# Attention scores with keys on partitions, 256 queries at a time, and the maximum taken elementwise

## The chip, the cores and the metric

The program runs on one core of one Trainium2 chip. The metric is the device time of one execution in microseconds (us). The kernel before was timed three times: median 3153.96 us, from 3151.37 to 3155.75.

The engines are named as in the profile: PE is TensorE (matmul and transpose), PEld its weight load, DVE is VectorE, ACT is ScalarE, POOL is GpSimd, SP is the queue that issues the DMAs. SBUF is the core's working memory, PSUM the memory that PE writes to; POOL's operands all lie in SBUF here.

## The reference

Two layers work on 1024 latent tokens and 256 context tokens of width 1024: a bidirectional gated recurrence and a multi-head attention whose keys and values come from a common 128-wide latent. The change lies in the attention, 16 heads, 1024 queries against 1280 keys:

```python
s = einsum('bqhd,bkhd->bhqk', q_nope, k_nope) + einsum('bqhr,bkr->bhqk', q_pe, k_pe)
p = softmax(s * MLA_SCALE, axis=-1)
o = einsum('bhqk,bkhd->bqhd', p, v)
y = (o * silu(z)) @ w_out
```

All of it is in float32.

## The kernel before

A float32 value is kept as two numbers of a shorter format (fp32r), a high and a low part, made by `split` (L209): ACT casts the high part, DVE subtracts it to give the low part. A product of two such numbers is three matmuls (`mm3`, L262). The projections of keys and queries are folded together, so that scores are taken straight against the key latent: `kh` and `kl` are its two parts, `kr` the rotary part, and a head's folded queries are `qah`, `qal` with the rotary parts `rh`, `rl`.

The first layer takes the first 1.7 ms. Then come its output projection and the input projections of the attention (`mla_in`, L669, `mla_rope`, `mla_z`), and from about 2142 us to 2960 us the attention itself (`attend`, L929), followed by the output projection.

`attn_scores` (L838) works on one tile of 128 queries of one head, queries on partitions and the 1280 keys along the free axis in blocks of 512, 512 and 256. Each block is five matmuls into one PSUM buffer `s` (L854 to L858). DVE reduces each block to a maximum (L860, as a minimum, since the scale carries a minus) and the three to one (L866). ACT takes the exponential with that number as its bias and sums the row as it goes (L870), and DVE forms the reciprocal and scales the whole row of 1280 (L876 to L881).

`attn_values` (L884) takes two tiles of one head, which I call a unit: 16 heads times 4 make 64 units. The scaled probabilities have queries on partitions, but the product with the values needs keys there. So PE transposes them, four 128x128 pieces at a time, into a PSUM buffer `pt` (L901), ACT and DVE split each group out of PSUM into `ph` and `pl` (L906, recorded at L215 and L216), and `mm3` adds ten key tiles into `pv` (L914). The result is copied and split again (L919 to L921, the last step `ol` on POOL), multiplied with the head's value weights (L924), by the gate `z` on DVE (L926), and stored (L927).

`attn_prep` (L782) makes the folded queries of the next head meanwhile: small weight products (L799), every second head the transposes of the rotary parts (L817), two groups of six 512-wide matmuls (L833) with their splits. `tail` stands for the first half of the output projection's work on the first two tiles, used to fill the end.

What sets the order: `attend` sorts all these steps by due times, and PE is held to exactly that order (`AT_ORDER`, L1283). The other engines' instructions are ordered by a scheduler. Every engine executes its own list in order and waits at an instruction whose inputs or buffers aren't ready.

Of the kernel before, what the change touches and what calls it, by code (L numbers as in the profile page):

```python
# [18 lines left out]
P = 128  # L19
# [18 lines left out]
class Net:  # L38
# [630 lines left out]
    def mla_in(self, pool, pp, kp, a, hh, hl, st):  # L669
# [6 lines left out]
        for c in range(NT):  # L676
# [39 lines left out]
            )  # L716
            if lat:
# [64 lines left out]
    def attn_prep(self, pool, pp, a, st, qrD, zT, h, box):  # L782
# [23 lines left out]
        if h % 2 == 0:  # L806
# [6 lines left out]
            for b, n in self.qgs:  # L813
                sl = slice(b * P, (b + n) * P)
                ps = t(pp, [P, 512], F32, G_TAG)
                for j in range(n):
                    nc.tensor.transpose(ps[:, j * P : (j + 1) * P], qr[:, b + j], self.ident)  # L817
                for i, (rh, rl) in enumerate(box["pair"]):
                    own, twin = (slice(0, 64), slice(64, P))[:: 1 - 2 * i]
                    src = ps[own, : n * P]  # L820
                    nc.scalar.activation(rh[own, sl], src, AF.Copy, scale=SCALE)
# [16 lines left out]
    def attn_scores(self, pool, pp, st, box, i, prs):  # L838
        nc, t, NT = self.nc, self.t, self.NT
        mm = nc.tensor.matmul  # L840
        LK = NT * P
        blocks = [(o, min(512, LK - o)) for o in range(0, LK, 512)]
        nb = len(blocks)
        h, j = divmod(i, self.NL)
        qah, qal, rh, rl = box[h][:4]
        js = slice(j * P, (j + 1) * P)
        mx = t(pool, [P, 4], F32, "mx")
        sm = t(pool, [P, 4], F32, "sm")
        pr = t(pool, [P, LK], F32, "pr")
        sc = []  # L850
        for b, (o, w) in enumerate(blocks):
            s = t(pp, [P, 512], F32, "s")
            ks = slice(o, o + w)
            mm(s[:, :w], qah[:, js], st["kh"][:, ks], start=True, stop=False)  # L854
            mm(s[:, :w], qah[:, js], st["kl"][:, ks], start=False, stop=False)  # L855
            mm(s[:, :w], qal[:, js], st["kh"][:, ks], start=False, stop=False)  # L856
            mm(s[:, :w], rh[:, js], st["kr"][:, ks], start=False, stop=False)  # L857
            mm(s[:, :w], rl[:, js], st["kr"][:, ks], start=False, stop=True)  # L858
            with self.tc.high_priority(offset=AT_PRIO):
                nc.vector.tensor_reduce(mx[:, b : b + 1], s[:, :w], AX.X, ALU.min)  # L860
            sc.append(s)
            if b < nb - 1:
                yield
        nm = t(pool, [P, 1], F32, "nm")
        with self.tc.high_priority(offset=AT_PRIO):
            nc.vector.tensor_reduce(nm, mx[:, :nb], AX.X, ALU.min)  # L866
        for b, (o, w) in enumerate(blocks):
            yield
            with self.tc.high_priority(offset=EXP_PRIO):
                nc.scalar.activation(  # L870
                    pr[:, o : o + w], sc[b][:, :w], AF.Exp, bias=nm, scale=-1.0,
                    accum_out=sm[:, b : b + 1],
                )
        yield
        rs = t(pool, [P, 1], F32, "rs")
        nc.vector.tensor_reduce(rs, sm[:, :nb], AX.X, ALU.add)  # L876
        nc.vector.reciprocal(rs, rs)
        if i % NORM_ACT[1] < NORM_ACT[0]:
            nc.scalar.activation(pr, pr, AF.Copy, scale=rs)
        else:  # L880
            nc.vector.tensor_scalar(pr, pr, rs, None, ALU.mult)  # L881
        prs[i] = pr

    def attn_values(self, pool, pp, st, box, u, prs, yT):  # L884
        nc, t, NT = self.nc, self.t, self.NT
        tiles = [i for i in (2 * u, 2 * u + 1) if i < self.NH * self.NL]
        h, b = divmod(tiles[0], self.NL)
        n = len(tiles)
        N = n * P
        wvh, wvl, z = box[h][4:]  # L890
        np_ = -(-NT // 2)
        parts = {}
        acc = None
        for e in range(np_ + PV_LAG):
            if e < np_:
                m = min(2, NT - 2 * e)
                tp = t(pp, [P, 2, 2 * P], F32, "pt")
                for c in range(m):
                    for j, i in enumerate(tiles):
                        k = 2 * e + c  # L900
                        nc.tensor.transpose(  # L901
                            tp[:, c, j * P : (j + 1) * P], prs[i][:, k * P : (k + 1) * P], self.ident
                        )
                ph = t(pool, [P, 2, 2 * P], F32R, "ph")
                pl = t(pool, [P, 2, 2 * P], F32R, "pl")
                self.split(ph[:, :m, :N], pl[:, :m, :N], tp[:, :m, :N])  # L906
                parts[e] = (m, ph, pl)
            if e >= PV_LAG:
                if acc is None:
                    acc = self.pv[:, u % 2]  # L910
                m, ph, pl = parts.pop(e - PV_LAG)
                for c in range(m):
                    k = 2 * (e - PV_LAG) + c
                    self.mm3(acc[:, :N], st["vh"][:, k], st["vl"][:, k], ph[:, c, :N], pl[:, c, :N], k == 0, k == NT - 1)  # L914
            yield
        oh = t(pool, [P, 2 * P], F32R, "oh")
        ol = t(pool, [P, 2 * P], F32R, "ol")
        o32 = t(pool, [P, 2 * P], F32, "o32")
        nc.scalar.copy(o32[:, :N], acc[:, :N])  # L919
        nc.scalar.copy(oh[:, :N], o32[:, :N])  # L920
# [469 lines left out]
```

## Time and profile before

| | |
|---|---|
| median of three runs | 3153.96 us (3151.37 to 3155.75) |
| the profiled execution, time | 3156.2 us |
| the profiled execution, span | 3154.4 us |
| TensorE clock granted, mean | 0.994 |
| busy: PE, PEld, DVE, ACT, POOL | 3115.5, 2783.9, 2150.9, 1727.9, 255.8 us |
| instructions | 51488 |
| 2142 to 2960 us: PE, DVE, ACT, POOL busy | 813.5, 638.2, 507.7, 65.4 of 818 us |

The span runs from the first to the last instruction; the execution's own time is 1.8 us longer. A busy PE is not a PE at its peak: matmuls overlap, so the recorded length of one (0.28 us) is longer than the distance to the next (0.12 us), and a sum must be made with the distances.

### The profile page before, as it was taken

What the parts mean: (1) busy time and instruction counts of PE and PEld (TensorE: products, weight loads), DVE (VectorE), ACT (ScalarE), POOL (GpSimd) and SP (SyncE); (2) the same over time, 40 slices, a digit from 0 to 9 for tenths busy, and PEclk for the clock granted to TensorE, in tenths of its full rate; (3) what the DMA queues carried; (4) which work ended last, traced back from release to release, by engine and by line L of the source; (5) the groups of instructions that cost most, each with busy time, mean ns of one, the idle gap of its engine ahead of it and who ended that gap; (6) DMA issues with size and microseconds to landing.
All of it is one profiled execution on the core that took longest, in us unless ns stands there. A gap on an engine that the chain in (4) does not pass through costs nothing.

```text
span 3154.4 us, 51488 instructions
## 1 busy us (share of the span) xinstructions
PE 3115.5 (99%) x19412; PEld 2783.9 (88%) x19412; DVE 2150.9 (68%) x4853; ACT 1727.9 (55%) x4263; POOL 255.8 (8%) x350
## 2 busy tenths in 40 slices
PE   8899999999999999999999999999999999999999
PEld 7889989889898998988988788788999999999887
DVE  7777688776886758767585463536777777777642
ACT  5556465564655646555475563324666666666532
POOL 2000000000000000000001122210000000000000
PEclk8999999999999999999999999999999999999999
DMA  5110212102121021110127561430111011101261
GB/s 212 42 56 24 73 36 63 56 23 74 36 62 56 25 65 36 37 35 23 41 68 242 193 205 59 140 119 29 41 30 38 21 38 31 35 29 38 69 219 57
DMA packets 100010, 218.88 MB, mean 69 GB/s; under 512 B 10289, under 2 KB 47409, under 8 KB 99761
## 3 DMA queue, kind: packets, MB, share of 16 engines
q1 hardware_dynamic: 99760, 215.59, 21.0%
q8 instruction: 153, 2.51, 0.3%
q14 instruction: 97, 0.79, 0.1%
HBM read 175.70 MB, written 39.85 MB: 68 GB/s over the span
## 4 chain that ended last, share of the span: by engine, by line
PE 88%; DVE 4%; DMA 2%; issue 2%; ACT 2%; POOL 1%; SPq 0%; DVEq 0%; POOLq 0%; ACTq 0%
PE g L265 11%; PE g L264 11%; PE g L266 11%; PE lv L336 6%; PE pt L901 4%; PE o L487 3%; PE pv L264 2%; PE s L854 2%; PE pv L265 2%; PE pv L266 2%; PE s L855 2%; PE s L857 2%; PE s L858 2%; PE s L856 2%; PE lv L264 2%
## 5 line engine op out<-in xcount | busy, mean ns | idle before, releaser
L264 PE MATMUL g<-hh,wh 128*128 128x512 f32 (+1 forms) x1512 | 548.7, 363 | 0.8 <-DVE hh L254 0.6
L266 PE MATMUL g<-hl,wh 128*128 128x512 f32 (+1 forms) x1512 | 542.0, 360 | 2.7 <-DVE hl L255 2.6
L265 PE MATMUL g<-hh,wl 128*128 128x512 f32 (+1 forms) x1512 | 543.3, 359 | 0.0
L216 DVE TENSOR_TENSOR wl<-raw,wh 128x1024 fp32r<-128x1024 f32 (+1 forms) x170 | 209.7, 1236 | 174.0 <-ACT wh L215 163.7
L266 PEld LDWEIGHTS g<-hl,wh 128*128 128x128 f32 x1512 | 286.0, 189 | 39.3 <-DVE hl L255 3.6
L264 PEld LDWEIGHTS g<-hh,wh 128*128 128x128 f32 x1512 | 286.7, 190 | 37.6 <-DVE hh L254 0.9
L265 PEld LDWEIGHTS g<-hh,wl 128*128 128x128 f32 x1512 | 286.6, 190 | 35.7
L860 DVE TENSOR_REDUCE mx<-s 128x1 f32<-128x512 f32 (+1 forms) x384 | 229.3, 598 | 93.7 <-PE s L858 92.6
L870 ACT ACTIVATE pr<-s,nm 128x512 f32<-128x512 f32 (+1 forms) x384 | 232.3, 613 | 99.3 <-DVE nm L866 93.1
L336 PE MATMUL lv<-QX,KX 128*128 128x128 f32 x1920 | 264.4, 276 | 6.0 <-ACT QX L408 3.5
L336 PEld LDWEIGHTS lv<-QX,KX 128*128 128x128 f32 x1920 | 247.8, 193 | 15.2 <-ACT QX L408 4.4
L215 ACT CAST wh<-raw 128x1024 fp32r<-128x1024 f32 (+1 forms) x170 | 177.7, 1049 | 120.2 <-PE lv L265 42.1
L215 ACT CAST ph<-pt 128x512 fp32r<-128x512 f32 x320 | 187.6, 586 | 95.2 <-PE pt L901 85.2
L216 DVE TENSOR_TENSOR pl<-pt,ph 128x512 fp32r<-128x512 f32 x320 | 219.1, 685 | 12.5 <-ACT ph L215 12.4
L264 PE MATMUL g<-wh,hh 128*128 128x256 f32 (+2 forms) x676 | 197.7, 293 | 0.0
L264 PE MATMUL pv<-ph,vh 128*128 128x256 f32 x640 | 196.6, 307 | 0.0
L266 PE MATMUL g<-wl,hh 128*128 128x256 f32 (+2 forms) x676 | 196.4, 291 | 0.0
L901 PE MATMUL pt<-ident,pr 128*128 128x128 f32 x1280 | 191.8, 272 | 0.1
L265 PE MATMUL g<-wh,hl 128*128 128x256 f32 (+1 forms) x654 | 187.8, 287 | 0.0
L408 ACT COPY KX<-K 128x256 f32<-128x256 f32 (+1 forms) x288 | 109.6, 381 | 133.1 <-PE lv L336 75.9
L266 PE MATMUL pv<-pl,vh 128*128 128x256 f32 x640 | 180.0, 281 | 0.0
L265 PE MATMUL pv<-ph,vl 128*128 128x256 f32 x640 | 179.8, 281 | 0.0
(557 smaller groups left out, 7956.6 us busy)
## 6 DMA issues: line engine op xcount, KB each, us to landing
raw<-in_w_o SPq DMA_DIRECT2D x64, 512.0 KB, 4.2
raw<-in_w_qfbz SPq DMA_DIRECT2D x61, 512.0 KB, 3.8
raw<-in_ada_wT SPq DMA_DIRECT2D x32, 512.0 KB, 3.6
raw<-in_w_mo SPq DMA_DIRECT2D x24, 512.0 KB, 4.0
raw<-in_w_v SPq DMA_DIRECT2D x16, 512.0 KB, 3.6
yT<-Z SPq DMA_DIRECT2D x32, 256.0 KB, 2.0
raw<-in_w_z SPq DMA_DIRECT2D x16, 512.0 KB, 3.9
pyr<-yT SPq DMA_DIRECT2D x64, 128.0 KB, 3.9
```

Source lines behind the costliest of these rows:

```text
L215: nc.scalar.copy(hi, src)
L216: (eng or nc.vector).tensor_tensor(lo, src, v32(hi), ALU.subtract)
L264: mm(ps, lh, rh, start=first, stop=False)
L265: mm(ps, ll, rh, start=False, stop=False)
L266: mm(ps, lh, rl, start=False, stop=last)
L336: nc.tensor.matmul(ps[:, sl], lhs[:, sl], rhs[:, sl], start=True, stop=True)
L408: cp(m12(N[:]), m12(Y))
L487: nc.tensor.matmul(o[:, sl], l, r, start=i == 0, stop=i == len(ops) - 1)
L854: mm(s[:, :w], qah[:, js], st["kh"][:, ks], start=True, stop=False)
L860: nc.vector.tensor_reduce(mx[:, b : b + 1], s[:, :w], AX.X, ALU.min)
L870: nc.scalar.activation(pr[:, o : o + w], sc[b][:, :w], AF.Exp, bias=nm, scale=-1.0, accum_out=sm[:, b : b + 1],)
L901: nc.tensor.transpose(tp[:, c, j * P : (j + 1) * P], prs[i][:, k * P : (k + 1) * P], self.ident)
```

## The change

Scores are now computed with keys on partitions, for a whole unit of 256 queries at a time, so that the probabilities come out as the product with the values wants them. No transposes of probabilities are left.

- **Scores.** Ten key tiles in five PSUM buffers of 512 columns (two tiles of 256 queries each; four called `s`, one `s5`, each there once). Four passes are made first: `kh` with `qah`, `kl` with `qah`, `kh` with `qal`, `kr` with `rh`.
- **Maximum.** DVE takes the elementwise maximum over the five buffers (`m2`: one copy, four maxima of 128x512), then of its halves (`mf`, 128x256). PE transposes `mf` (two 128x128 pieces into `mt`), DVE reduces to one number for each query (`mr`), two matmuls with the identity spread it over a row, and ACT writes the negative into row 64 of the low rotary part `rl`.
- **Fifth pass.** A new operand `k5` holds the rotary keys in rows 0 to 63 and ones in row 64. The fifth pass, `k5` with `rl`, thus adds the low part and subtracts the maximum. It comes after the maximum is known.
- **Exponential and sums.** ACT takes the exponential of five buffers of 512 with no bias and no row sums. POOL adds the five up (four adds of 128x512, one of 128x256) to `l`; two float32 matmuls with a column of ones sum `l` over keys. Probabilities are no longer scaled; DVE takes the reciprocal `rc` of 128x2, SP writes it to DRAM (`lD`) and reads it back spread over all partitions (`rb`), and POOL multiplies the gated output `ya` by it.
- **Split.** `attn_split` makes `ph` and `pl` straight from the exponentials in SBUF.
- **Order.** `attend` is written out as a loop over units: scores of unit u, with splits of unit u-1 and the values of unit u-2 between them. DVE and ACT are now held to the written order too (`AT_HAND`).
- In `mla_in` ACT makes one more copy of 64x128 for each of ten key tiles.

The diff, cut to its core:

```diff
+            nc.scalar.copy(st["k5"][:64, sl], tp[:64, P : 2 * P])
...
+        for e in range(nb):
+            s = t(pp, [P, 512], F32, "s" if e < 4 else "s5")[:, : 2 * N].rearrange("p (a q) -> p a q", a=2)
+            for c in range(m):
+                for i, (l, r) in enumerate(((kh, qah), (kl, qah), (kh, qal), (kr, rh))):
+                    mm(o, l[:, ks], r[:, js], start=c + i == 0, stop=c == m - 1 and i == 3)
-                nc.vector.tensor_reduce(mx[:, b : b + 1], s[:, :w], AX.X, ALU.min)
+                    nc.vector.tensor_tensor(m2[:, :m], m2[:, :m], s[:, :m], ALU.max)
...
+                nc.vector.tensor_tensor(mf, m2[:, 0], m2[:, 1], ALU.max)
+            nc.tensor.transpose(mt[:, 0, j * P : (j + 1) * P], mf[:, j * P : (j + 1) * P], self.ident)
+            nc.vector.tensor_reduce(mr, mt[:, 0, :N].rearrange("p (j k) -> p j k", k=P), AX.X, ALU.max)
+            mm(mt[:, 1, j * P : (j + 1) * P], mr[:, j : j + 1].broadcast_to([P, P]), self.identr, ...)
+            nc.scalar.activation(rl[64:65, js], mt[64:65, 1, :N], AF.Copy, scale=-1.0)
+                mm(s[:, c], st["k5"][:, ks], rl[:, js], start=False, stop=c == m - 1, skip_group_check=True)
-                    pr[:, o : o + w], sc[b][:, :w], AF.Exp, bias=nm, scale=-1.0,
-                    accum_out=sm[:, b : b + 1],
+                nc.scalar.activation(p[:, :m], s[:, :m], AF.Exp)
+            add(l2, whole[0], whole[1], ALU.add)
+                add(l2, l2, p, ALU.add)
+            add(l, l2[:, 0], l2[:, 1], ALU.add)
...
-                        nc.tensor.transpose(
-                            tp[:, c, j * P : (j + 1) * P], prs[i][:, k * P : (k + 1) * P], self.ident
-                        )
-                self.split(ph[:, :m, :N], pl[:, :m, :N], tp[:, :m, :N])
+        self.split(ph[:, :m], pl[:, :m], p[:, :m])
...
+        nc.vector.reciprocal(rc, ps[:, 2 * P : 2 * P + n])
+        nc.sync.dma_start(row.rearrange("o (j p) -> p (o j)", p=P), rc)
+        nc.sync.dma_start(rb, row.broadcast_to([P, N]))
+        nc.gpsimd.tensor_tensor(y, y, rb, ALU.mult)
```

**DVE's list, before.** These are the rows of DVE over one tile of 128 queries, half a unit, in the middle of a head: block maxima `mx`, their minimum `nm`, sum and reciprocal `rs`, the scaling of the row `pr`, low parts `pl` taken from `pt` (PSUM) and `ph`.

```order
L860 TENSOR_REDUCE mx_27045<-s_27048 128x1
L926 TENSOR_TENSOR ya_27063<-pt_27059,za_5047_26022 128x256
L876 TENSOR_REDUCE rs_27055<-sm_26962 128x1
L877 RECIPROCAL rs_27055<-rs_27055 128x1
L881 TENSOR_SCALAR pr_26963<-pr_26963,rs_27055 128x1280
L216 TENSOR_TENSOR pl_27072<-pt_27066,ph_27071 128x512
L860 TENSOR_REDUCE mx_27045<-s_27081 128x1
L216 TENSOR_TENSOR pl_27094<-pt_27088,ph_27093 128x512
L860 TENSOR_REDUCE mx_27045<-s_27103 128x1
L866 TENSOR_REDUCE nm_27110<-mx_27045 128x1
```

**DVE's list, after.** These are the rows of DVE over one unit with no preparation of a next head in it: the running maximum `m` (the tile `m2`), its halves `mf`, the number for each query `mr`, and `pl`, now from `p` and `ph`, which both lie in SBUF.

```order
L864 COPY m_5172_27081<-s_27082 128x512
L862 TENSOR_TENSOR m_5172_27081<-m_5172_27081,s_27092 128x512
L862 TENSOR_TENSOR m_5172_27081<-m_5172_27081,s_27102 128x512
L216 TENSOR_TENSOR pl_27113<-p_27050,ph_27112 128x512
L862 TENSOR_TENSOR m_5172_27081<-m_5172_27081,s_27116 128x512
L216 TENSOR_TENSOR pl_27127<-p_27054,ph_27126 128x512
L862 TENSOR_TENSOR m_5172_27081<-m_5172_27081,s_5181_27130 128x512
L872 TENSOR_TENSOR mf_27141<-m_5172_27081 128x256
L216 TENSOR_TENSOR pl_27144<-p_27058,ph_27143 128x512
L878 TENSOR_REDUCE mr_27167<-mt_27140 128x2
L216 TENSOR_TENSOR pl_27170<-p_27062,ph_27169 128x512
L216 TENSOR_TENSOR pl_27174<-p_27066,ph_27173 128x512
```

Two low parts now stand between the block maxima, ahead of `mf`, and a third between `mf` and `mr`; the scaling of the rows is gone.

**POOL's list, before.** Over five units POOL has one `ol` for each and, every second head, the copies of the rotary part.

```order
L921 TENSOR_TENSOR ol_25320<-o_4881_25321,oh_25319 128x256
L825 COPY qrh_4905_25404<-qrh_4905_25404 64x512
L825 COPY qrh_4906_25405<-qrh_4906_25405 64x512
L921 TENSOR_TENSOR ol_25517<-o_4930_25518,oh_25516 128x256
L921 TENSOR_TENSOR ol_25691<-o_4970_25692,oh_25690 128x256
```

**POOL's list, after.** One unit: the sums `l` over the exponentials `p`, the product `ya` by the reciprocal `rb`, and `ol`.

```order
L903 TENSOR_TENSOR l_4986_26211<-p_26192,p_26196 128x512
L959 TENSOR_TENSOR ya_26177<-ya_26177,rb_26175 128x256
L905 TENSOR_TENSOR l_4986_26211<-l_4986_26211,p_26200 128x512
L943 TENSOR_TENSOR ol_26218<-o_4989_26219,oh_26217 128x256
L905 TENSOR_TENSOR l_4986_26211<-l_4986_26211,p_26204 128x512
L905 TENSOR_TENSOR l_4986_26211<-l_4986_26211,p_26208 128x512
L909 TENSOR_TENSOR l_26210<-l_4986_26211 128x256
```

The step that PE waits for at the head's value weights, `ol`, was alone on its engine. Now it stands behind two sums and behind `ya`, which waits for the DMA that brings `rb`.

More of the change, by code (lines that the diff above doesn't have):

```diff
@@ L916, in attn_values @@
[L916 to L920, printed above, removed]
[L921 removed]
+        acc = self.pv[:, u % 2]
+        k = 0
+        for m, ph, pl in cell["parts"]:
+            for c in range(m):
+                self.mm3(acc[:, :N], st["vh"][:, k], st["vl"][:, k], ph[:, c], pl[:, c], k == 0, k == NT - 1)
+                k += 1
+            yield
@@ L934, in attend @@
-        steps = []
+        units = [(h, b, min(2, NL - b)) for h in range(NH) for b in range(0, NL, 2)]
+        nb = -(-self.NT // 2)
+        per = -(-NL // 2)
+        prep = {}
         for h in range(1, NH):
-            t0 = NL * (h - 1) + 3 + AT_LAG
-            g = self.attn_prep(pool, pp, a, st, qrD, zT, h, box)
-            gap = min(0.9, (NL - 4 - AT_LAG) / 5)
-            steps += [(t0 + (e + (PREP_LATE if e > 1 and h % 2 == 0 else 0)) * gap, g) for e in range(6)]
-        nb = -(-self.NT * P // 512)
@@ L956 @@
+        for x in vals.values():
+            for _ in x:
+                pass
+        for _ in tail:
+            pass
 VEC = {}
```

237 lines of the change are left out of this document (144 added, 93 removed).

## Prediction

> **What bounds the kernel now.** I read the stages first (busy time in stretches), then the chain of waits inside a stretch of the attention, then the groups by line, then POOL and DVE in order of time, and last the DMA issues. In the stages, the columns are length, then busy time of PE, PEld, DVE, ACT and POOL, then granted clock and DMA:
>
> ```profile
> 2142.00:2960.00 818.00, 813.47 (x5524) 742.30 (x5523) 638.18 (x1361) 507.72 (x1306) 65.38 (x90) 1.00 0.10 31
> ```
>
> PE has no idle time to speak of in the attention, and POOL has little else. The chain of waits of 2446 to 2460 us, with its shares by line and some of its pieces (start, length, what), is PE alone:
>
> ```profile
> by line: PE pt L901 18.7%; PE s L856 10.8%; PE pv L266 10.3%; PE pv L264 10.2%; PE pv L265 10.2%; PE s L855 10.1%; PE s L854 9.9%; PE s L858 9.2%; PE s L857 9.2%; PE pt L266 0.9%; PE pt L264 0.8%; PE pt L265 0.8%
> ...
> 2446.18 0.12 PE s L858
> 2446.30 0.44 PE pt L901 x4
> 2446.74 0.12 PE pv L264
> ...
> 2447.46 0.23 PE s L854
> ```
>
> So a matmul of 256 columns holds PE for 0.12 us, one of 512 for 0.23, and a group of four transposes of probabilities for 0.44. POOL's `ol` comes once a unit and so gives the period (start, length, engine, line):
>
> ```profile
> 2343.16 0.73 POOL L921 TENSOR_TENSOR ol<-o,oh 128x256 fp32r<-128x256 f32 x1 [11.84 <-PE s L858]
> ...
> 2446.31 0.73 POOL L921 TENSOR_TENSOR ol<-o,oh 128x256 fp32r<-128x256 f32 x1 [11.82 <-PE s L858]
> 2458.22 0.74 POOL L921 TENSOR_TENSOR ol<-o,oh 128x256 fp32r<-128x256 f32 x1 [11.18 <-ACT oh L920]
> ```
>
> Two heads, eight units, take 2446.31 - 2343.16 = 103.15 us, 12.9 a unit; a unit without preparation of a head takes 11.9.
>
> **The change: PE.** All counts are per unit. The score passes are 30 matmuls before (2 tiles x 5 x (0.235 + 0.235 + 0.12) = 5.9 us, with 0.235 for the 512 columns) and 50 of 256 columns after (50 x 0.12 = 6.0): the columns are the same, and narrower passes cost 0.1 more. The other matmuls that stay are 30 for the values (3.6) and three for the head's value weights (0.36). Five groups of transposes go: 5 x 0.44 = 2.2. Together that makes 12.06 where the rows show 11.9, so the distances account for the unit. New are two transposes of `mf` (half a group, 0.22, up to 0.3 with the change of format), two matmuls of 128 columns that spread the maximum (bounded by two of 256 columns, 0.24), and the two sums by a column of ones. A float32 matmul counts as two instructions here. The nearest row is the two-column matmul of the start, 15 in 1.81 us:
>
> ```profile
> 39.85 1.81 PE L163 MATMUL lv<-csil,adap 128*128 128x2 f32 x15
> ```
>
> That is 0.12 each, four are 0.48. Net: -2.2 + 0.1 + 0.3 + 0.24 + 0.48 = -1.08 us a unit; a head's preparation is unchanged. Eight units would take 103.15 - 8.6 = 94.5 us if PE were still never idle, and the 64 units would win 69 us. That is the ceiling.
>
> **DVE and ACT.** The costs come from these groups (line, operation, count, busy us, mean ns):
>
> ```profile
> L216 DVE TENSOR_TENSOR pl<-pt,ph 128x512 fp32r<-128x512 f32 x320 | 219.1, 685 | 12.5 <-ACT ph L215 12.4
> L860 DVE TENSOR_REDUCE mx<-s 128x1 f32<-128x512 f32 x256 | 175.5, 686 | 77.9 <-PE s L858 76.8
> L860 DVE TENSOR_REDUCE mx<-s 128x1 f32<-128x256 f32 x128 | 53.9, 421 | 15.9 <-PE s L858 15.9
> L881 DVE TENSOR_SCALAR pr<-pr,rs 128x1280 f32<-128x1280 f32 x128 | 113.1, 884 | 3.2
> L407 DVE TENSOR_TENSOR QX<-QX,Ta 128x256 f32<-128x256 f32 x96 | 40.1, 418 | 0.0
> L570 ACT ACTIVATE Z<-g 128x512 f32<-128x512 f32 x32 | 19.1, 598 | 87.7 <-PE g L266 87.6
> L365 ACT CAST UH<-U 128x512 fp32r<-128x512 f32 x16 | 9.9, 620 | 3.7 <-DVE U L362 3.7
> ```
>
> DVE loses four block reductions of 0.69, two of 0.42 and two scalings of 0.88 (5.4), and gains five maxima of 0.69 (the copy taken like them), `mf` and `mr` at 0.42 (4.3). ACT's five exponentials cost 0.6 each without sums, the casts 0.62 from SBUF. Both stay well under PE's time. Their totals don't decide; what does is that three results now come back to PE inside one unit. PE and DVE in order of time (start, length):
>
> ```profile
> 2521.04 0.28 PE L858 MATMUL s<-kr,qrl 128*128 128x256 f32 x1
> ...
> 2521.36 0.42 DVE L860 TENSOR_REDUCE mx<-s 128x1 f32<-128x256 f32 x1 [0.16 <-PE s L858]
> ```
>
> Count from the first score matmul of a unit without preparation:
>
> - Blocks of eight end every 0.95 us; DVE starts 0.2 later (below, 2521.36 less 2521.04 and 0.12). With 0.61 between DVE starts (the low part at 2446.69 in the rows below is followed at 2447.30), the third maximum starts at 3.03, then low part, maximum, low part, maximum: `mf` runs 6.2 to 6.6. PE has 40 score matmuls (4.75) and 18 value matmuls (2.1), so it wants `mf` at 6.85. Margin 0.25.
> - `mr` follows one low part; PE wants it 1.6 after the transposes (values 0.72, ones 0.48, value weights 0.36), and DVE needs 0.2 to start and 0.42. Margin some 0.9.
> - ACT writes the row of `rl` while PE does the last values step, 0.7: just hidden. The first buffer is free for the next unit when its exponential ends, 0.12 + 0.2 + 0.6 after the fifth pass began; the pass lasts 1.2.
>
> With preparation of a head, DVE waits in its list for ACT's casts of the folded queries (PE 1.4, then ACT 0.6, then DVE 0.69). `mf` then ends at 8.3 where PE wants it at 8.25: no margin. So every delay on DVE ahead of `mf` goes straight to PE.
>
> **POOL against DVE.** Such a delay comes from the sums on POOL. Here are DVE and POOL in order of time during the input projections, then in the attention:
>
> ```profile
> 2019.55 1.21 DVE L216 TENSOR_TENSOR wl<-raw,wh 128x1024 fp32r<-128x1024 f32 x1
> 2020.68 1.51 DVE L216 TENSOR_TENSOR ql<-q,qh 128x256 fp32r<-128x256 f32 x1
> ...
> 2019.77 2.15 POOL L756 TENSOR_TENSOR zst<-zst,t 128x512 f32<-128x512 f32 x1 [5.13 <-DVE t L755]
> ...
> 2446.69 0.69 DVE L216 TENSOR_TENSOR pl<-pt,ph 128x512 fp32r<-128x512 f32 x1
> 2447.30 0.15 DVE L866 TENSOR_REDUCE nm<-mx 128x1 f32<-128x3 f32 x1
> ```
> ```profile
> L756 POOL TENSOR_TENSOR zst<-zst,t x16: 1284/1292/2152, 1981.4 to 2085.6; 128x512 f32<-128x512 f32 x16
> ```
>
> POOL's add of 128x512 takes 1.29 us alone (the median). Begun behind DVE's subtraction of two SBUF operands it took 2.15: it stood still until DVE was done at 2020.76, and DVE's next one, 0.42 long by its size, took 1.51 because it stood still until POOL was done at 2021.92. They exclude each other for the whole instruction. The low part of 2446.69, whose one input lies in PSUM, ran its 0.69 while POOL's `ol` of 2446.31 ran its 0.73: these don't. The Trainium skill (SBUF — State Buffer, section "Who interferes with whom") says this as a rule: a VectorE instruction with two SBUF inputs contends with a GpSimd instruction that reads SBUF, and one with a single SBUF input doesn't. The trace agrees on both halves (2.15 against 1.29; 0.69 and 0.73 undisturbed), and the rule speaks against this change.
>
> The change takes the low parts' first input from PSUM to SBUF and gives POOL 4 x 1.29 + 3 x 0.74 = 7.4 us of work a unit (four sums, the sum of halves, `ya`, `ol`). Five low parts and `mf` meet it. A DVE instruction that comes at a random moment waits on average (4 x 1.29 x 1.29 + 3 x 0.74 x 0.74) / (2 x 12.9) = 0.32 us, at most 1.29. Three of them lie ahead of `mf` (two low parts and itself): 1.0 us, less the margin of 0.25 in a plain unit, and 1.0 whole in a unit with preparation. The one ahead of `mr` is worse than random, since POOL has been held off by `mf` and comes next: up to 1.29 against a margin of 0.9, so 0.4. I take 0.6 of stall for a plain unit (some of its waits fall where margins take them) and 1.0 + 0.4 = 1.4 for one with preparation, from bounds of 0 and 2.6 (two full waits). In two heads there are five with preparation (three slots of two steps for an even head, two for an odd) and three plain: 5 x 1.4 + 3 x 0.6 = 8.8 us. That is the whole gain: 94.5 + 8.8 = 103.3.
>
> **DMAs.** Added per unit are the write of `lD` and the read of `rb`, the second waiting on SP for the first. Nearest are these (KB each, median us to landing):
>
> ```profile
> yT<-ya SPq DMA_DIRECT2D x64, 128.0 KB, 1.8
> za<-zT SPq DMA_DIRECT2D x16, 512.0 KB, 3.6
> qr<-qrD SPq DMA_DIRECT2D x8, 512.0 KB, 4.4
> ```
>
> So 1.8 each at least, and up to 4.4 for the write, whose 256 numbers of 4 bytes lie apart, and 3.6 for a read queued behind `za`. I take 2 and 2. `za`, `wk` and `qr` queue behind them on SP, but are wanted units later. POOL, however, waits in its list at `ya`, and `l` and `ol` queue behind it. The circle is: value weights, `rc` (behind the last low parts on DVE, about 1.2), two DMAs 4.0, `ya` 0.74, a sum 1.29, `ol` 0.74, and value weights again with 0.6: 8.6, plus POOL's and DVE's mutual waits of 1 to 2. That is under 12.9 and doesn't bind; late ones cost an estimated 0.5 us per eight units, 4 in all.
>
> **The rest.** The last unit's `ya` comes 4 us of DMA later, under output matmuls of the first tiles that don't need it; I keep 3 (0 to 6). The ten copies in `mla_in` lie on ACT, which is half idle there: 0, with 5 either way for the scheduler's new interleaving. Sum: 3156.2 + 8 x (103.3 - 103.15) + 4 + 3 = 3164, against the profile's own execution; the median of the runs lies 2.2 lower, so **3162 us**.
>
> **Rivals.**
>
> - *The waits miss the path* (faster). POOL's sums fall beside the maxima, whose one input lies in PSUM, and low parts slip between. For it: DVE has 4.3 us of such work per unit. Against: POOL needs 7.4. With 0.3 us of stall left per unit: 3154 - 69 + 19 = 3104.
> - *The circle through DRAM binds* (slower). If the 4-byte write lands late, `ol` keeps PE waiting at the value weights. It decides once the two DMAs take more than about 7 us together (12.9 less 4.6 for the rest of the circle and 1.2 of mutual waits). Written at 4.4 and read behind `za` at 3.6, the circle is 8.6 + 4 + 1.2 = 13.8 a unit: 64 x 0.9 = 58 more, 3212. Against: writes of rows landed in 1.8.
> - *No transposes' worth to win*: narrower passes cost more than half. Rows of 0.12 and 0.23 exclude it; I give it nothing.
>
> **How the numbers follow.** The forecast, with stalls of 0.8 to 1.4 a unit, has 0.50 (3140 to 3190); the missed waits 0.28, the circle or heavier stalls 0.22. A measurement can tell about 0.2%, 6.3 us, from no change: 3147.7 to 3160.3. Of the forecast's half, 0.08 lies below that, 0.16 in it, 0.26 above. Faster: 0.28 + 0.08 = 0.36; same 0.16; slower 0.22 + 0.26 = 0.48. The range runs from a little above the first rival's 3104 to the second's 3212: 3108 to 3212.
>
> **What would show it.** Right: PE idle ahead of the `mt` transposes (released by `mf`) and ahead of the spread (released by `mr`), some 1 us a unit; low parts and POOL's sums with maxima far above their 0.69 and 1.29; no transposes of probabilities. The circle: PE idle ahead of the value weights, released by `ol`, and POOL idle for DMA `rb`. Wrong: low parts at 0.69 throughout and a unit near 12.0, or score passes not at 0.12.

## The result, and the profile after

The changed kernel takes 3480.6 us (median of four runs, 3478.1 to 3484.4) beside 3152.7 us of the kernel before: 1.104 times as long, 95% interval 1.1028 to 1.1055. The forecast was 3162 us with a range up to 3212, so the result lies far outside on the slow side. The mechanism is that of the second rival, the circle through DRAM.

First, where the time lies. These are the score passes of before and of after (minimum, median and longest matmul in ns, then first and last start), the spans being 3154.4 and 3479.9 us:

```profile
L854 PE MATMUL s<-kh,wl x384: 277/394/505, 2142.8 to 2958.0; 128*128 128x512 f32 x128, 128*128 128x256 f32 x64
```
```profile
span 3479.9 us, 52947 instructions
...
L858 PE MATMUL s<-wl,kh x640: 276/281/415, 2145.7 to 3220.7; 128*128 128x256 f32 x160
```

I cut every span at these two starts. Before: 2142.8 us up to the first score, 815.2 of attention, 196.4 from the last score pass to the end. After: 2145.7, 1075.0, 259.2. The 325.5 us more are 2.9 ahead of the attention, 259.8 in it and 62.8 behind it. This division isn't quite even: by their counts and 0.12 us each, an estimate, the changed kernel leaves some 16 us of the attention's matmuls behind it and the kernel before 12.5, so some 4 us stand in the end that before has in the attention.

The page of after and the waits of 2300 to 3100 us (engine, line, waited for: us in total, times, longest) show what PE waits for:

```profile
POOL 2000000000000000000112221444444444444100
PEclk8999999999999999999999998888888888888799
...
PE 65%; issue 12%; DMA 12%; POOL 6%; DVE 4%; ACT 1%; POOLq 0%; SPq 0%; DVEq 0%; ACTq 0%
...
L266 PE MATMUL pt<-ol,wvh 128*128 128x256 f32 x64 | 31.5, 493 | 191.9 <-POOL ol L943 191.9
```
```profile
PE pt L266 <- POOL ol L943: 145.0, 46, 5.4
```

DMA stands in the chain that ended last with 12%. In these 800 us PE waits 46 times, 3.2 us each, at the value weights for `ol`. The chain of waits of 2606 to 2624 us goes once round (start, length, what):

```profile
by line: DMA lD<-rc 47.1%; DMA rb<-lD 27.1%; POOL l L905 9.3%; PE pt L266 6.6%; POOL ol L943 6.3%; POOL ya L959 4.1%; issue 1.5%; DVE ya L958 0.5%; DVE rc L952 0.3%; POOLq L959 0.2%; SPq L956 0.1%; POOLq L905 0.1%
...
2605.90 0.59 PE pt L266
...
2606.72 8.49 DMA lD<-rc
...
2615.27 4.87 DMA rb<-lD
...
2620.31 0.74 POOL ya L959
2621.04 1.68 POOL l L905
2622.72 1.14 POOL ol L943
...
2623.91 0.60 PE pt L266
```

From one value-weight matmul to the next are 18.01 us, of which the two transfers are 13.36 and the rest is 4.65. The transfers' landing times in 2300 to 3100 us (KB each, median us):

```profile
za<-zT SPq DMA_DIRECT2D x12, 512.0 KB, 12.9
rb<-lD SPq DMA_DIRECT2D x46, 128.0 KB, 5.0
yT<-ya SPq DMA_DIRECT2D x46, 128.0 KB, 1.7
...
lD<-rc SPq DMA_DIRECT2D x46, 1.0 KB, 8.5
```

The write of 1 KB takes 8.5 us, the store of 128 KB 1.7. `za`, 3.6 before, takes 12.9 behind them. PE in order of time shows a second loss:

```profile
2602.39 0.28 PE L265 MATMUL pt<-oh,wvl 128*128 128x256 f32 x1
2605.90 0.58 PE L266 MATMUL pt<-ol,wvh 128*128 128x256 f32 x1 [3.24 <-POOL ol L943]
...
2611.19 0.41 PE L858 MATMUL s<-wl,kl 128*128 128x256 f32 x1
2611.40 0.41 PE L858 MATMUL s<-wh,kh 128*128 128x256 f32 x1
...
2612.50 0.28 PE L858 MATMUL s<-wl,kh 128*128 128x256 f32 x1
2612.62 0.28 PE L858 MATMUL s<-wl,kl 128*128 128x256 f32 x1
```

Behind a wait of 3.24 us the distance of the matmuls is 0.21 for some 6 us, then 0.12 again: half clock, which the row PEclk shows as 0.8 in the mean. It costs next to nothing of its own here, because PE waits for the circle anyway; where the circle is gone it does cost.

### The profile page after: what moved, and what is told of

The parts are those of the page before. It is cut to its first block, busy times and chain, and to the rows that moved or that the text cites. A ratio compares the mean times of both kernels' runs of the same rounds, so it can differ in the third digit from the quotient of the medians.

```text
span 3479.9 us, 52947 instructions
## 1 busy us (share of the span) xinstructions
PE 3191.6 (92%) x19924; PEld 2898.4 (83%) x19924; DVE 2074.6 (60%) x4473; ACT 1674.2 (48%) x3889; POOL 687.3 (20%) x734
## 4 chain that ended last, share of the span: by engine, by line
PE 65%; issue 12%; DMA 12%; POOL 6%; DVE 4%; ACT 1%; POOLq 0%; SPq 0%; DVEq 0%; ACTq 0%
PE g L264 11%; PE g L265 11%; PE g L266 11%; DMA lD<-rc 8%; PE lv L336 6%; PE o L487 3%; DMA rb<-lD 2%; PE lv L264 2%; PE lv L265 2%; PE lv L266 2%; PE s L858 2%; POOL l L905 2%; PE o L452 2%; POOL ol L943 1%; POOL ya L959 1%
## 5 line engine op out<-in xcount | busy, mean ns | idle before, releaser
L81 POOL TENSOR_SCALAR rsq_m<-oss 128x4 f32<-128x4 f32 (+1 forms) x48 | 26.3, 548 | 1532.5 <-ACT ojunk L491 1532.5
L905 POOL TENSOR_TENSOR l<-l,p 128x512 f32<-128x512 f32 x192 | 256.0, 1333 | 7.0
L216 DVE TENSOR_TENSOR pl<-p,ph 128x512 fp32r<-128x512 f32 x320 | 237.1, 758 | 5.6 <-ACT ph L215 5.4
L886 ACT ACTIVATE qrl<-mt 1x256 fp32r<-1x256 f32 x64 | 24.0, 375 | 405.0 <-PE mt L881 289.7
L215 ACT CAST ph<-p 128x512 fp32r<-128x512 f32 x320 | 179.2, 619 | 67.2 <-PE pv L265 65.5
L266 PE MATMUL pt<-ol,wvh 128*128 128x256 f32 x64 | 31.5, 493 | 191.9 <-POOL ol L943 191.9
L864 DVE COPY m<-s 128x512 f32<-128x512 f32 x64 | 44.3, 692 | 267.9 <-PE s L858 267.9
L895 ACT ACTIVATE p<-s 128x512 f32<-128x512 f32 x320 | 163.7, 608 | 83.2 <-PE s L892 81.7
L266 PE MATMUL g<-wl,hh 128*128 128x256 f32 (+2 forms) x676 | 196.4, 291 | 0.0
L858 PE MATMUL s<-wl,kh 128*128 128x256 f32 x640 | 193.1, 302 | 0.0
```

What stands on the lines that cost most here:

```text
L215: nc.scalar.copy(hi, src)
L216: (eng or nc.vector).tensor_tensor(lo, src, v32(hi), ALU.subtract)
L266: mm(ps, lh, rl, start=False, stop=last)
L858: mm(o, l[:, ks], r[:, js], start=c + i == 0, stop=c == m - 1 and i == 3)
L864: nc.vector.tensor_copy(m2[:, :m], s[:, :m])
L895: nc.scalar.activation(p[:, :m], s[:, :m], AF.Exp)
```

## The experiments

Theory: the period is the circle of `rc`, two transfers, `ya`, a sum, `ol` and the value weights. Rivals: the small pieces load the DMA engines, so that traffic and not a wait is what costs; and DVE's and POOL's mutual exclusion is far larger than forecast. In the table, attention and end are cut as above and are those of the one profiled execution, which can lie some us off the median (3182.0 beside 3178.8 in e2_nodma); ratios are to the kernel before, with their intervals.

| kernel | us | ratio | attention | end |
|---|---|---|---|---|
| before | 3152.7 | 1 | 815.2 | 196.4 |
| after | 3480.6 | 1.1041 (1.1028 to 1.1055) | 1075.0 | 259.2 |
| e1_unread | 3211.3 | one run | 815.4 | 246.7 |
| e2_nodma | 3178.8 | 1.0074 (1.0057 to 1.0091) | 815.5 | 219.1 |
| e3_row | 3209.0 | one run | 836.9 | 224.9 |
| e4_spread | 3204.9 | 1.0160 (1.0145 to 1.0175) | 832.2 | 224.8 |
| e5_late | 3127.3 | 0.9913 (0.9896 to 0.9929) | 760.6 | 217.2 |
| e6_nosum | 3129.3 | 0.9919 (0.9900 to 0.9937) | 760.2 | 216.9 |
| e7_warm | 3169.3 | 1.0046 (1.0031 to 1.0061) | 800.3 | 219.1 |
| e8_lagged | 3437.2 | 1.0904 (1.0889 to 1.0918) | 1036.0 | 252.6 |
| e9_laglate | 3298.8 | 1.0464 (1.0449 to 1.0478) | 891.7 | 258.6 |
| e10_splits | 3304.4 | one run | 895.7 | 259.1 |
| e11_held | 3358.9 | 1.0649 (1.0632 to 1.0667) | 965.1 | 249.5 |
| e12_heldlate | 3367.6 | 1.0679 (1.0663 to 1.0695) | 968.4 | 252.4 |
| e13_held3 | 3237.5 | 1.0271 (1.0255 to 1.0287) | 843.9 | 242.0 |
| e14_heldlate3 | 3149.2 | 0.9981 (0.9972 to 0.9990) | 753.2 | 246.9 |
| e15_end | 3135.8 | 0.9947 (0.9933 to 0.9960) | 752.1 | 232.4 |

### Is it the round trip?

**e1_unread**: the transfers are made, but POOL multiplies by a constant tile of ones instead of `rb`, so the output isn't normalised.

```diff
-        nc.gpsimd.tensor_tensor(y, y, rb, ALU.mult)
+        nc.gpsimd.tensor_tensor(y, y, self.one[:, :N], ALU.mult)
```

> Both DMAs (lD and rb) are still issued for every unit, but POOL multiplies ya by a tile of ones that is set once, so nothing waits for rb; the output is left unnormalised. Theory A (the round trip through DRAM, 8.5 us for lD and 5.0 for rb, stands ahead of the sums and of ol in POOL's list and makes the period): POOL's wait before ya goes from 9 us to under 1, the unit falls from 17.4 to about 13 us, the clock of the attention returns to 1.0, the time is 3130 to 3190. Theory B (POOL's sums and DVE's low parts exclude each other and that is most of the loss): POOL's work is the same as before, so the time stays above 3400. Theory C (the 256 scattered 4-byte writes themselves disturb other transfers): the time stays above 3300, with za and qr landing as late as now (12.9 and 7.0 us).

**e2_nodma**: the same, with the transfers not issued at all.

> As the one before, and lD and rb aren't issued at all; the output is left unnormalised. Theory A: within 10 us of the run with unread DMAs, 3130 to 3190, and what is left against the kernel before is the mutual exclusion of POOL and DVE that was forecast: PE idle ahead of the mt transposes and the spread, about 1.1 us a unit. Theory B: above 3400. Theory C: 100 us or more below the run with unread DMAs.

The score passes of e1_unread and the landing time of its write in 2300 to 3100 us:

```profile
L858 PE MATMUL s<-wl,kh x640: 276/282/415, 2147.4 to 2962.8; 128*128 128x256 f32 x160
```
```profile
lD<-rc SPq DMA_DIRECT2D x56, 1.0 KB, 8.3
```

With POOL's wait gone the attention takes 815.4 us instead of 1075.0, although `lD` still lands in 8.3: the wait is what costs there, and the transfers as such cost the attention nothing (815.5 without them). They do cost 27.6 us behind the last score pass, which I had not expected: e1_unread lies 21 us above its range, and the two kernels differ by 32.5 us and not by 10. The first rival thus doesn't explain the attention. At the end it is only one of two candidates, because e1_unread keeps a wait on SP, that of each read for its write: between 2955 and 3060 us SP stands still for 37.5 us in five such waits, and weight loads of the output projection stand behind them.

**e3_row**: the sum is formed as one row on one partition, so that `lD` is written as one run of 1 KB; the read and the wait for it stay.

```diff
+        nc.tensor.matmul(ps[:1, 2 * P : 2 * P + N], self.ones, cell["l"], start=True, stop=True)
...
+        rc = t(pool, [1, N], F32, "rc")
+        nc.vector.reciprocal(rc, ps[:1, 2 * P : 2 * P + N])
...
+        nc.sync.dma_start(row, rc)
```

> The sums are taken as one row of 256 on one partition (ones as the stationary operand), the reciprocal is taken of that row, and lD is written as one run of 1 KB instead of 256 pieces of 4 bytes; rb is read and waited for as now. Theory A with the pieces as the cause of the 8.5 us: lD lands in about 2 us, the circle falls from 17.9 to 11.5 us plus what the reciprocal of a row of 256 costs on DVE (0.3 to 2 us), so the unit is 13 to 14 us and the time 3170 to 3240. If the 8.5 us were the price of any write followed by a wait on SP, lD stays at 8 us and the time at 3450 or above. Theory B: no change, above 3400.

SP and DVE of this kernel in order of time:

```profile
2621.11 0.23 SPq L951 DMA_DIRECT2D lD<-rc  x1
2622.21 0.32 SPq L953 DMA_DIRECT2D rb<-lD  x1
```
```profile
2608.19 1.74 DVE L949 RECIPROCAL rc<-pt 1x256 f32<-1x256 f32 x1
```

The read, which waits on SP for the write, is issued 1.1 us behind it where it was 8.5 in after: the same 1 KB in one piece. So the 256 pieces of 4 bytes are the price of the write. They also slow the transfers beside them: by its packets in the trace, a load of `za` takes some 2.9 us in e3_row, about as before, and 12 to 14 in after. The circle no longer binds (836.9). That isn't the write's doing alone, though: the scheduler has put `ya` behind `ol` in POOL's list here (`ol` at 2624.35, `ya` at 2625.38), where after has it ahead. e10_splits, below, has the same order with the slow write and the late low parts, and takes 895.7. And the reciprocal of a row of 256 takes 1.74 us where 128x2 took 0.17, and that goes to DVE: in 2300 to 2800 us PE waits 36.1 us for `mf`, 26.4 in e2_nodma.

**e4_spread**: no DRAM; PE spreads `rc` over the partitions with two float32 matmuls one unit later, and DVE multiplies. It computes everything.

```diff
+            nc.tensor.matmul(
+                sb[:, j * P : (j + 1) * P], rc[:, j : j + 1].broadcast_to([P, P]), self.ident, start=True, stop=True
+            )
+        nc.vector.tensor_tensor(y, y, sb[:, :N], ALU.mult)
```

> No DRAM: the reciprocal of 128x2 is spread over all partitions by two float32 matmuls with the identity, one unit later, and DVE multiplies ya by it from PSUM; POOL loses ya and keeps the sums and ol. Normalised output. Theory A: PE gains about 0.5 us a unit against the run without DMAs (four instructions of 128 columns), DVE 0.4, POOL loses 0.74: 3120 to 3190, beside the kernel before. Theory B: about 10% less POOL work, so above 3350.

The attention is 16.7 us longer than without normalising at all, and the end 5.7. That is a price of work, not of waits, since PE waits for `mf` 25.5 us in 2300 to 2800 us, no more than there. It is 15 us above the range that I expected, and still slower than before.

### What is left without the circle?

Without DMAs the attention takes as long as before (815.5 and 815.2), as the forecast had it: 103.3 us for eight units forecast, 103.0 to 104.6 between PE's `mt` transposes of e2_nodma. (A plain unit is below one without preparation of a head.) Its stalls, POOL and DVE in order of time:

```profile
2604.12 3.43 POOL L905 TENSOR_TENSOR l<-l,p 128x512 f32<-128x512 f32 x2
```
```profile
2605.22 1.18 DVE L216 TENSOR_TENSOR pl<-p,ph 128x512 fp32r<-128x512 f32 x1
2606.33 0.67 DVE L862 TENSOR_TENSOR m<-m,s 128x512 f32<-128x512 f32 x1
2607.04 0.79 DVE L872 TENSOR_TENSOR mf<-m 128x256 f32<-128x256 f32 x1
```

Two adds take 3.43 instead of 2.6, a low part 1.18 instead of 0.68, `mf` 0.79 instead of 0.42; the maximum from PSUM between them keeps its 0.67. Next, the same trace's windows (length, busy PE, PEld, DVE, ACT, POOL, granted clock, DMA) behind a wait of 1.86 us for `mf` that ended at 2518.65:

```profile
2518.50:2520.00 1.50, 1.35 (x12) 1.35 (x12) 1.50 (x4) 0.00 (x0) 0.00 (x0) 0.94 0.00 0
2520.00:2521.50 1.50, 1.50 (x8) 1.50 (x8) 1.07 (x4) 0.00 (x0) 0.89 (x1) 0.50 0.01 5
2521.50:2523.00 1.50, 1.50 (x8) 1.50 (x8) 0.18 (x1) 0.38 (x1) 0.74 (x1) 0.50 0.00 0
2523.00:2524.50 1.50, 1.50 (x14) 1.50 (x13) 0.00 (x0) 1.13 (x3) 0.00 (x0) 0.93 0.26 87
```

Here the clock is halved for some 3.4 us, beginning 1.2 us after the wait has ended. Three kernels take this apart; all are e2_nodma with one edit more, and none normalises.

**e5_late**: the low parts of a unit, all but one, move behind `mr`.

```diff
-SPLIT_AT = (2, 3)
+SPLIT_AT = ()
```

> The kernel without the two DMAs (3178.8 us), with all but one of the low parts of a unit moved behind the reduction that gives each query's maximum; the output is again not normalised. Theory: what is left of PE's waiting, 0.6 us in a plain unit and up to 1.9 us in one with preparation, comes from low parts that stand ahead of the halves' maximum on DVE, each stretched by POOL's sums. Then the waits go (5.5 us in eight units) and with them the half clock behind the longest (some 3 us in eight units): 3178.8 less about 60, 3110 to 3130 us. Rival: the maxima themselves and the wait for ACT's casts in the preparation make PE wait, or the low parts come too late for the values: 3165 to 3185 us.

54.9 us less in the attention: shown. Eight units take 96.1 to 96.7 us, and PE waits for `mf` only once in them (0.83 to 1.06).

**e6_nosum**: POOL's four adds of 128x512 are left out.

```diff
...
-            add(l2, whole[0], whole[1], ALU.add)
-            for p in whole[2:]:
-                add(l2, l2, p, ALU.add)
...
+        l2 = whole[0]
```

> The kernel without the two DMAs, with POOL's four adds of 128x512 left out, so that the sum covers two of ten key tiles; not normalised. Theory (DVE and POOL exclude each other): low parts at 0.65 to 0.7 us instead of up to 1.3, the halves' maximum at 0.42 instead of 0.79, so the waits of 0.6 us in plain units go and the long ones fall by half: 3120 to 3145 us. Rival (the order of DVE's list alone makes the waits): waits stay within 0.2 us of what they are, 3165 to 3180 us.

The low parts of e2_nodma and then of this kernel (minimum, median, longest in ns):

```profile
L216 DVE TENSOR_TENSOR pl<-p,ph x320: 676/684/1685, 2164.9 to 2987.0; 128x512 fp32r<-128x512 f32 x160
```
```profile
L216 DVE TENSOR_TENSOR pl<-p,ph x320: 679/683/693, 2164.7 to 2930.8; 128x512 fp32r<-128x512 f32 x160
```

No low part exceeds 0.69 any more, where e2_nodma had up to 1.69, and the attention falls by 55.3 us. So the exclusion does it, and standing out of its way is worth as much as removing the sums. This is the rule of the Trainium skill that the prediction weighed (SBUF — State Buffer, "Who interferes with whom"), and it held.

**e7_warm**: 14 matmuls whose result is overwritten fill PE's longest wait, in the first two units and in one unit of eight.

```diff
+        for j in range(cell["fill"]):
+            mm(mt[:, 1, :N], kh[:, :P], qah[:, js], start=True, stop=True)
```

> The kernel without the two DMAs, with 14 matmuls of 256 columns, whose result is overwritten, in the place where PE waits longest for the halves' maximum: the first two units and every unit in which a pair of heads' rotary queries is prepared. Nothing else is changed, and the wait is as long as before. Theory: PE runs at half clock for some 7 us after each such wait because it stood idle for 1.9 us; with the gap filled the distance stays 0.12 us behind it, and 3 us are won in each of nine places: 3178.8 less some 25, 3150 to 3158 us. Rival: the half clock has another cause than the idle time (load, or the unit's work): no change, 3175 to 3185 us.

The granted clock of 2400 to 2800 us rises from 0.98 to 1.00 and the median falls by 9.5 us, well under half of what I expected: the cause is shown, my price was too high. I had taken 3 us a place from an occurrence of 6.8 us. In the trace of e2_nodma five of the nine stretches of half clock last 6.8 us and four 3.4; at a distance of 0.21 instead of 0.12 they cost some 3 and 1.5 us, an estimate, and two of 3.4 us are left in e7_warm. The profiled executions fit that, with 15.2 us less in the attention. But the profiled one is the slowest of e2_nodma's four, which run from 3175.9 us at a granted clock of 0.987 to 3182.0 at 0.984: it seems that the half clock isn't equally long in each execution.

The Trainium skill (TensorE: Matmul & The Clock Gate, "Part 1: The HAM clock gate") has half rate follow an idle window of about 3.4 us. The lengths of 3.4 and 6.8 us agree with one or two such windows; the idle time doesn't. In e2_nodma half clock followed on all six waits of 1.84 to 1.86 us between 2300 and 2840 us, in e6_nosum on one of six waits of 1.56 us, and on none of 0.6 to 0.9 in the plain units.

### Can the round trip be kept?

**e8_lagged** and **e9_laglate**: the read is written one unit after the write, the multiplication another unit later; e9_laglate has the late low parts too. Both have four buffers of `ya` instead of two; with three of `rc` and `rb` besides, a first form (e8_lag), the attention's tiles need 94.2 KB a partition of SBUF where 93.4 are left, and there is no time of it.

```diff
+        y = t(pool, [P, N], F32, "ya")
+        nc.vector.tensor_tensor(y, ps[:, :N], z[:, b * P : b * P + N], ALU.mult)
+        yield
         rb = t(pool, [P, N], F32, "rb")
         nc.sync.dma_start(rb, row.broadcast_to([P, N]))
-        y = t(pool, [P, N], F32, "ya")
-        nc.vector.tensor_tensor(y, ps[:, :N], z[:, b * P : b * P + N], ALU.mult)
+        yield
         nc.gpsimd.tensor_tensor(y, y, rb, ALU.mult)
```

> The changed kernel with its two DMAs kept, the read issued one unit after the write and POOL's multiplication one unit after that. Theory: the price of the round trip was the place of the waits, on POOL ahead of the sums and on SP ahead of every later load; with both gone the kernel comes down to the one without the DMAs (3178.8) plus a few us: 3180 to 3192 us. Rival: the traffic of 256 pieces of 4 bytes slows the other transfers itself, as in the kernel that reads the row and doesn't use it: 3205 to 3215 us.

> Both repairs in one kernel that computes everything: the two DMAs a unit apart and POOL's multiplication another unit later, and the low parts behind the maximum. Theory: the two prices are independent, so this is the kernel with late low parts (3127.3) plus what the lagged DMAs cost: 3128 to 3145 us, faster than the kernel before. Rival: late low parts or the DMA traffic take the gain back: 3150 to 3185 us.

**e10_splits**: the changed kernel with `SPLIT_AT = ()` alone.

> The changed kernel with the low parts behind the maximum and nothing else changed. Theory: while the circle through DRAM sets the period, relief on DVE wins nothing that reaches PE, since PE's wait for the maximum is spent ahead of the same wait for the value weights: 3470 to 3485 us. Rival: the two waits add up, and this wins the 52 us that it won without the DMAs: 3425 to 3435 us.

All three refute what I expected of them. In e8_lagged POOL's and SP's lists, which the scheduler orders, have the multiplication back in front of a sum and `ol`, and the read as SP's first issue behind the write that waits for it: the lag stands in the program and not in the queues. And e10_splits, where I expected nothing, wins 176 us, since POOL's list now has `ya` directly behind `ol`, with five sums between it and the next `ol`, instead of just ahead of it. Its chain of waits of 2600 to 2630 us shows what binds then:

```profile
2599.67 0.76 POOL ya L959
...
2600.45 0.32 SPq L960
...
2600.86 7.94 DMA lD<-rc
...
2608.82 4.92 DMA rb<-lD
...
2613.90 0.75 POOL ya L959
...
2614.67 0.32 SPq L960
...
2615.04 6.76 DMA lD<-rc
```

This is a second circle without PE in it: SP's list has the store of `ya` ahead of the next write, so write, read, multiplication, store, next write take 14.2 us a unit. My prediction knew only the first.

**e11_held** and **e12_heldlate** (the latter with late low parts) hold POOL to the written order too and let ACT issue the read.

```diff
-AT_HAND = {mybir.EngineType.PE, mybir.EngineType.DVE, mybir.EngineType.Activation}
+AT_HAND = {mybir.EngineType.PE, mybir.EngineType.DVE, mybir.EngineType.Activation, mybir.EngineType.Pool}
...
-        nc.sync.dma_start(rb, row.broadcast_to([P, N]))
+        nc.scalar.dma_start(rb, row.broadcast_to([P, N]))
```

> The changed kernel with its two DMAs kept; POOL's list is held in the written order too (the sums of a unit, then the value step's low part, then the multiplication for a unit two before), and the read is issued by ACT behind the next unit's exponentials, a unit after the write, so that neither POOL nor SP has a wait for a transfer in flight. Theory: the two earlier kernels with the read a unit later failed because the scheduler put the multiplication back between sums and low part and the read back behind the write; two circles bind, one through POOL and PE, one through SP alone (write, read, multiplication, store, next write: 14 us). With both open the kernel comes down to the one without the DMAs: 3178 to 3200 us. Rival: small pieces load the DMA engines themselves, or the sums in front of the low part make PE wait: 3205 to 3300 us.

> The same with the low parts behind the maximum. Everything of the reference is computed. Theory: 52 us less, as without the DMAs: 3126 to 3148 us, faster than the kernel before by 0.2 to 0.9%. Rival: with everything of the sums in front, POOL's low part of the value step comes late behind the low parts on DVE, or the traffic costs: 3150 to 3250 us.

Refuted again, by a wait that I made. The waits of e12_heldlate in 2300 to 2900 us:

```profile
POOL l L909 <- PE pt L947: 177.1, 39, 7.0
...
PE pt L266 <- POOL ol L943: 79.4, 39, 2.1
```

POOL's last sum writes a buffer that PE's ones matmuls free only just ahead of the value weights, and in the written order `ol` stands behind that sum. So **e13_held3** and **e14_heldlate3** give `l` a third buffer, and `ya` three instead of four. The lines show them against the two kernels above.

```diff
-"l": 2, ... "ya": 4,
+"l": 3, ... "ya": 3,
```

> The kernel with POOL's list held and the read a unit later, with three buffers for the sum of halves instead of two. Theory: nothing of the round trip is left on a path, so the kernel comes down to the one without the DMAs, 3178.8 and up to 20 more for ol standing behind all sums: 3175 to 3200 us. Rival: the small pieces' traffic or the write's place on SP still costs: 3205 to 3300 us.

> The same with the low parts behind the maximum; everything of the reference is computed. Theory: 52 us less, as without the DMAs: 3123 to 3148 us, faster than the kernel before by 0.2 to 0.9%. Rival: another wait takes their place: over 3150 us.

The score passes of e14_heldlate3, and its landing times in 2300 to 2900 us:

```profile
L858 PE MATMUL s<-wl,kh x640: 279/281/415, 2147.9 to 2901.1; 128*128 128x256 f32 x160
```
```profile
rb<-lD ACTq DMA_DIRECT2D x51, 128.0 KB, 8.0
za<-zT SPq DMA_DIRECT2D x12, 512.0 KB, 11.9
...
lD<-rc SPq DMA_DIRECT2D x51, 1.0 KB, 8.6
```

The transfers are slower than ever, 16.6 us together, and the attention takes 753.2 us, the least so far. POOL still waits for `rb`, 30.1 us in 2300 to 2800 us, but PE waits for `ol` no more: a round trip that PE doesn't wait for costs the attention nothing. The time, 3149.2 us, is 1.2 above the range that I expected. (e13_held3 stays at 843.9 and above its forecast, as the sums, now in a row, meet the early low parts: PE waits 1.4 us for `mf` in many plain units, where e2_nodma had 0.6.) The end takes 246.9 us, as in e1_unread: SP has three weight loads of the output projection behind a store of the last units, which waits for their round trip:

```profile
2956.72 0.39 SPq L954 DMA_DIRECT2D lD<-rc  x1
2972.34 0.32 SPq L962 DMA_DIRECT2D yT<-ya  x1
2972.75 1.36 SPq L287 DMA_DIRECT2D raw<-in_w_mo  x3
```

Between the first two of these lines SP issues nothing for 15 us.

**e15_end**: POOL issues the transfers of the last two units: write, read and store.

```diff
+        last = u >= self.NH * -(-self.NL // 2) - 2
...
+        (nc.gpsimd if last else nc.sync).dma_start(row.rearrange("o (j p) -> p (o j)", p=P), rc)
...
+        (nc.gpsimd if last else nc.scalar).dma_start(rb, row.broadcast_to([P, N]))
...
+            nc.gpsimd.dma_start(yT[h][:, b * P : b * P + N], y)
```

> The repaired kernel (three buffers, late low parts; everything of the reference is computed) with the write, the read and the store of the last two units issued by POOL, which has nothing else to do there. Theory: at the end three weight loads of the output projection stand on SP behind the store of the last units, which waits for the last round trip; off SP they come some 20 us earlier, and PE's idle time of 2956 to 2980 us goes: 3149.2 less 15 to 25, 3124 to 3134 us. Rival: the end is slow because the small pieces load the DMA engines, or because the last heads' output itself is late: within 5 us of 3149.

The end falls by 14.5 us and the time by 13.4 (from 0.9981 to 0.9947 of the kernel before), short of the 15 to 25 expected. ACT still waits 36.8 us behind the last score pass for weights. So the place of these transfers in the queues is about half of what the round trip costs there, 29.7 us beside e5_late, which has none; how much of the rest is traffic stays open. This version computes everything and is faster than the kernel before: 0.9947 (0.9933 to 0.9960).

## Why the prediction was wrong, point by point

- **PE's work: right.** Forecast 1.08 us less in a plain unit, 10.8; e15_end has plain units of 10.6 to 10.7. The ceiling of 69 us was nearly there: its attention is 63.1 us shorter than before, some 4 of them by the uneven division.
- **The mutual stalls: right in sum, by other parts.** Forecast 8.8 us in eight units. Measured in e2_nodma: 5.5 of waits for `mf` (0.6 in plain units as forecast), 0.9 for the rotary queries' low part `qrl`, and the rest half clock behind the longest wait; the last two I did not foresee, so the sum is in part luck. The wait for `mr`, forecast at 0.4 in a unit with preparation, is 1.0 us in the whole attention.
- **The DMAs: the step that failed.** "I take 2 and 2", hence a circle of 8.6 that "doesn't bind". Measured 8.49 and 4.87. The rest of the circle, 4.6 forecast, is 4.65, but by errors that cancel: the sum and `ol` take 1.68 and 1.14 us instead of 1.29 and 0.74, the way from the value weights to the write 0.8 instead of 1.8. The bound of about 7 us for both transfers, from which the rival decides, held: 13.36 binds. What was wrong is the 2 for the write and its upper bound: 4.4 was the row of a load of 512 KB, near to this write neither in bytes nor in pieces. The read passed its bound too, 4.87 against 3.6. The 256 pieces lay in the diff, and the prediction names them, but no row of before showed such a write. The page's packets show them now:

```profile
DMA packets 100010, 218.88 MB, mean 69 GB/s; under 512 B 10289, under 2 KB 47409, under 8 KB 99761
```
```profile
DMA packets 126640, 227.44 MB, mean 65 GB/s; under 512 B 28720, under 2 KB 74032, under 8 KB 126384
```

The difference under 512 B, 18431, is 288 for each of 64 units: 256 for the write's elements, and 16 for each of the two transfers, as the transfers of before have them too (1216 for 76 in 2300 to 2900 us). The Trainium skill (DMA: Bandwidth & Descriptors, "Rules for kernel authors") says that a strided last dimension becomes one descriptor per element; the packets agree. It gives no price for such a write, and I had not weighed it.

- **The end: failed too.** Forecast 3 (0 to 6), measured 62.8, some 4 of them by the uneven division. Of the 62.8, 22.7 remain without any DMA (e2_nodma), where PE has gaps and half clock while the last two units' values drain; what would close them I have not tried. 27.6 come with the unread transfers, by SP's waits and by slower weight loads (5.7 us to landing instead of 4.6), in shares that no run separates, and the last 12.5 with the waits of the changed kernel.
- **The start** was given 0 with 5 either way: 2.9.
- **The rivals.** The second named the mechanism, the place and the sign. Its price was capped at 58 us by the same wrong bound; measured are 259.8 in the attention. The first, missed waits, did not come: the waits were there.

## What to carry to other kernels

Where a step leaves an engine and comes back through DRAM, draw every circle that it closes, through each in-order queue it touches, the DMA queue with its stores among them, and give the transfer the price of its pieces, not of its bytes; if no row shows pieces of that size, leave the upper end open. A lag that stands only in the program is none: read it in the order of each queue, and count the buffers behind which the moved step now stands. A step that starts a chain of waits at the end of a stage also delays the next stage's loads on the same queue.

## What the hardware showed that I had not expected

- 1 KB written as 256 pieces of 4 bytes lands in 8.5 us; as one run, the next transfer could be issued 1.1 us later. Other transfers slow down beside such writes: `za` from 3.6 to 12.9 us to landing.
- Waits of 1.84 to 1.86 us were enough to halve PE's clock, for 3.4 or 6.8 us, beginning 0.5 to 1.8 us after the wait's end.
- A reciprocal on DVE of a 1x256 row takes 1.74 us, of 128x2 0.17: of the same 256 values, the longer row is the dearer.
